# Layer 1's norm from x with features on partitions, in a two-layer retention / latent-attention trunk

## The chip, the cores and the metric

One core of a Trainium2 chip runs the whole program in one launch. The metric is the device time of one execution in microseconds (us). Engines are named as the profile names them: PE is TensorE's matrix products and PEld its weight loads, DVE is VectorE, ACT is ScalarE, POOL is GpSimd, SP is SyncE, which here only issues loads.

## The reference, cut to what matters

The model has two layers over a sequence of 512 tokens with 2048 features, batch 1. The first layer ("layer 1" in this document, index 0 in the code) is a retention layer, the second an attention layer. Each normalises x, shifts and scales it by vectors made from a conditioning vector c, and projects the result h.

```
def rmsnorm(x, g):
    y = x * rsqrt(mean(x * x, axis=-1) + EPS)          # one factor for each token
    return y * g

c_act = silu(c)
for i in range(2):
    shift, scale, gate = split(c_act @ ada_w[i] + ada_b[i], 3)
    h = rmsnorm(x, norm_g[i]) * (1.0 + scale) + shift
    y = retention_branch(h, ...) if i == 0 else mla_branch(h, ...)
    x = x + gate * y
return rmsnorm(x, final_norm_g)
```

In `retention_branch`, `h @ w_in` projects the 2048 features to q and k (2048 columns each), v and a gate g (4096 each). All is computed in float32; the kernel gets that precision on TensorE by splitting each operand into a high and a low part and adding three products (high x high, high x low, low x high).

## The kernel before, in words

The change concerns the first stage, which makes h for layer 1 and at the same time multiplies it with the first head's weights. h is held with features on partitions: 16 tiles `hT[kt]` of 128 features by 512 tokens, each with a high and a low half.

**Units.** The stage goes through 8 units of two tiles (kt = 2u and 2u+1). In each unit three sets of weights are used: "qk" (4 PSUM banks of results), "v" (4 banks) and "g" (3 banks). `products(kind, kt)` issues, for each bank, the three products of one tile; a unit has 24 + 18 + 24 = 66 products of 512 columns. There are eight PSUM banks (4 called `acc`, 4 called `aux`). The g banks stay; qk and v take turns in the four `acc` banks: after the first set (`here`) and g, `swap` copies its four partial results to SBUF (L379) and copies the other set's back (L383), both on ScalarE, and then `bank_products` does the second set (`there`). The next unit begins with the set that is already in the banks.

**Preparing a unit.** While TensorE multiplies unit u, `prepare_ahead(u+1)` prepares the next one. In the order of issue it does the following: ScalarE casts the weights of `here` to their high part (L330); VectorE reduces one tile of the modulation matrix against c (`sum_mod`, L353, once for shift and once for scale of each kt), makes the low part of the last odd h (L246) and the low part of `here` (L332), and reduces the second modulation tile; then `make_first` makes two columns, `b_col` (L366) and `a_col` (L367), on VectorE, and ScalarE makes h twice from the transposed x (`make_h`, L243 and L245). Then follow g's cast and low part, the cast of `there`, and two more reductions. After `swap`, `prepare_behind` makes the odd tile's h and the low part of `there`.

**The norm of x.** x comes in with tokens on partitions, as eight loads (L428). `square(t)` sums the squares of each token along the free axis, one half on ScalarE (L463) and one on VectorE (L464). `rsqrt` (L126) makes the factor: one small operation on VectorE (L129) and a power on POOL (L131). `diagonal(t)` (L476) writes the factors onto a diagonal matrix, and `transpose(kt)` (L497) multiplies four 128 x 128 blocks of x with these diagonals on TensorE, which transposes and normalises at once; ScalarE copies the result to SBUF (L502). Six tiles are transposed before the first product, tile 6 and 7 within unit 0, and two more in each of units 1 to 4.

**Order.** `queued(f)` puts the instructions of f behind the last ones already issued on ScalarE, VectorE, TensorE and SP, so the program's order is the order of each engine's queue. Buffers are taken from rings; those that matter are the raw weights (3), the high and low weights (3 each for qk and v, 4 named `k4b` for g), the modulation tiles `aw` (4, of 1 MB) and the tiles `k4` (8, x transposed). A load on SP waits for its buffer, and so do all loads behind it.

Of the kernel before, what the change touches and what calls it, by code (L numbers as in the profile page):

```python
# [49 lines left out]
def hybrid_trunk_kernel(  # L50
# [44 lines left out]
    def big(name, dt=F32R):  # L95
        return base.tile([P, 2, T], dt, tag="big", bufs=16, name=name)
# [4 lines left out]
    def k4b(name, dt=F32R):  # L101
        return base.tile([P, 2, T], dt, tag="k4b", bufs=4, name=name)
# [10 lines left out]
    def small(name, n=1):  # L113
        return base.tile([P, n], F32, tag="small", bufs=24, name=name)
# [248 lines left out]
    def make_first(kt):  # L363

        k1 = slice(kt, kt + 1)
        DVE.tensor_add(b_col[0][:, k1], mods[kt, 0], bias_c[0][:, k1])  # L366
        DVE.scalar_tensor_tensor(  # L367
            out=a_col[0][:, k1], in0=mods[kt, 1], scalar=bias1[:, k1], in1=norm_c[0][:, k1], op0=ALU.add, op1=ALU.mult
        )
        hT[kt] = big(f"hT_{kt}")  # L370
        return make_h(0, kt, xT[kt // 2][:, kt % 2, :], hT[kt])

# [18 lines left out]
    def product(kind, kt, b, late):  # L391
        lhs, rhs = first_sets[kind][1](loaded[kind, kt // 2], kt, b)
        passes = [(0, 0), (0, 1), (1, 0)]
        low = passes.pop(2 if kind == "v" else 1)
        for i, j in (low,) if late else passes:
            PE.matmul(
                banks[kind][b], lhs[i], rhs[j], start=kt == 0 and i + j == 0, stop=kt == KD - 1 and late,
                skip_group_check=True,
            )

    def bank_products(kind, u):

        for b in range(first_sets[kind][0]):
            for kt in (2 * u, 2 * u + 1):
                for late in (False, True):
                    product(kind, kt, b, late)

    A_, V_, T_, S_ = (getattr(mybir.EngineType, e) for e in ("Activation", "DVE", "PE", "SP"))

# [10 lines left out]
    def queued(fn, *args):  # L420
        with behind(A_, V_, T_, S_):
            return fn(*args)


    xs = [[big(f"x_{t}_{j}", F32) for j in range(2)] for t in range(NT)]
    for t in range(NT):
        for j in range(2):
            nc.sync.dma_start(  # L428
                xs[t][j], x[t * P : (t + 1) * P, j * 1024 : (j + 1) * 1024].rearrange("p (a b) -> p a b", a=2)
            )  # L430
# [12 lines left out]
    mods[1, 0] = queued(load_mod, 1, 0)  # L443
    load_first("qk", 0)
# [11 lines left out]

    bias1 = l0p.tile([P, KD], F32, name="bias1")

    ss = [small(f"x_ss_{t}", 2) for t in range(NT)]
    norm = [None] * NT  # L460

    def square(t):
        ACT.activation(k4b(f"x_sq_{t}_0", F32), xs[t][0], AF.Square, accum_out=ss[t][:, 0:1])  # L463
        DVE.scalar_tensor_tensor(  # L464
            out=k4b(f"x_sq_{t}_1", F32), in0=xs[t][1], scalar=1.0, in1=xs[t][1], op0=ALU.mult, op1=ALU.mult,
            accum_out=ss[t][:, 1:2],
        )
        s1 = small(f"x_s1_{t}")
        DVE.tensor_add(s1, ss[t][:, 0:1], ss[t][:, 1:2])
        norm[t] = rsqrt(s1, 1, 1.0 / D, f"x_{t}")  # L470

    diags = []

    def diagonal(t):
        diags.append(l0p.tile([P, P], F32, tag="diag", bufs=4, name=f"x_diag{t}"))
        DVE.tensor_scalar(out=diags[t], in0=ident, scalar1=norm[t], scalar2=None, op0=ALU.mult)  # L476

    tables_d = dram.tile([4 * P, T], F32, name="tables_d")
    ret_tables = [rot(l0p, f"ret_{n}") for n in ("cos", "sin")]
    tables = rotary_tables(*ret_tables, 0, False, "ret", ACT)  # L480
    for t in range(NT):
        queued(square, t)
        queued(silu, t)
        if t > 0:
            queued(diagonal, t - 1)
    queued(diagonal, NT - 1)
    POOL.dma_start(c_d, c_all[0:1, :])
    low_v = queued(prepares["v", 0])
    queued(lambda: DVE.tensor_scalar(out=bias1, in0=bias_c[0][:, KD:], scalar1=1.0, scalar2=None, op0=ALU.add))

    xT = [k4(f"xT_{u}", F32) for u in range(NU)]

    def transpose(kt):

        ps = aux(f"xT_ps_{kt}")
        for t in range(NT):
            PE.matmul(  # L497
                ps[:, t * P : (t + 1) * P],
                xs[t][kt // 8][:, (kt % 8) // 4, (kt % 4) * P : (kt % 4 + 1) * P],
                diags[t], start=True, stop=True,  # L500
            )
        return lambda: ACT.copy(xT[kt // 2][:, kt % 2, :], ps)  # L502
# [48 lines left out]
    queued(sum_mod, 1, 1)  # L551
    swap(None, "v")
    queued(products, "v", 0)
# [4 lines left out]
    queued(products, "qk", 0)  # L558
    prepare_ahead(1, low)
    queued(products, "qk", 1)  # L560
    queued(queued(transpose, 6))
    queued(products, "g", 1)
    queued(swap, "qk", "v")
    low = prepare_behind(1)
    queued(queued(transpose, 7))
    queued(products, "v", 1)
    for u in range(1, NU):

        here, there = ("qk", "v") if u % 2 == 0 else ("v", "qk")
        more = u + 1 < NU  # L570
        ahead = [2 * u + 6, 2 * u + 7] if 2 * u + 7 < KD else []
        if more:
            load_unit(u + 1)
            prepare_ahead(u + 1, low)
# [6 lines left out]
        for kt in ahead[:1]:  # L581
            queued(queued(transpose, kt))
        for kt in (2 * u, 2 * u + 1):
            queued(products, "g", kt)
        if more:
# [13 lines left out]
        for kt in ahead[1:]:  # L599
            queued(queued(transpose, kt))  # L600
    qk0, g0 = banks["qk"], banks["g"]
    l0.__exit__(None, None, None)

# [1569 lines left out]
```

## Time and profile before

| what | value |
|---|---|
| median of 3 runs | 2192.07 us (2192.05 to 2193.84) |
| profiled execution: its own time | 2192.7 us |
| its span | 2190.9 us |
| PE busy | 2160.2 us (99%) |
| DVE busy | 1557.4 us (71%) |
| ACT busy | 1013.1 us (46%) |
| POOL busy | 102.5 us (5%) |
| DMA moved | 440.26 MB, mean 201 GB/s |
| transposes of x | 64 products of 128 x 128, 128 instructions, 12.3 to 116.2 us |
| first product of v | 26.16 us |
| last product of the first stage | 161.42 us |

The span is the time from the first to the last instruction in the profile; the run's time lies 1.8 us around it. A busy share is the mean over stages with different limits, so the change has to be read in its own stage, the first 162 us. In lines of the timeline the first two numbers are the start and the length in us, the brackets give how long the engine had been idle and what ended that; "x8" counts instructions that follow each other. Lines of groups give the count, the total in us, the mean in ns and the idle time ahead.

### The profile page before, as it was taken

What the parts mean: (1) busy time and instruction counts of PE and PEld (TensorE: products, weight loads), DVE (VectorE), ACT (ScalarE), POOL (GpSimd) and SP (SyncE); (2) the same over time, 40 slices, a digit from 0 to 9 for tenths busy, and PEclk for the clock granted to TensorE, in tenths of its full rate; (3) what the DMA queues carried; (4) which work ended last, traced back from release to release, by engine and by line L of the source; (5) the groups of instructions that cost most, each with busy time, mean ns of one, the idle gap of its engine ahead of it and who ended that gap; (6) DMA issues with size and microseconds to landing.
All of it is one profiled execution on the core that took longest, in us unless ns stands there. A gap on an engine that the chain in (4) does not pass through costs nothing.

```text
span 2190.9 us, 27827 instructions
## 1 busy us (share of the span) xinstructions
PE 2160.2 (99%) x10280; PEld 1805.1 (82%) x10280; DVE 1557.4 (71%) x2345; ACT 1013.1 (46%) x1529; POOL 102.5 (5%) x178
## 2 busy tenths in 40 slices
PE   7999999999999999999999999999999999999997
PEld 5887888888888878888888888898788889888887
DVE  7878867676676788756677767667877677776545
ACT  5664434434343444434344545344444366664443
POOL 0000000000000000010000000010000000000000
PEclk9999999999999999999999999999999999999998
DMA  9965785867768678574645556453458723235323
GB/s 382 346 246 166 231 295 181 271 214 238 247 197 278 220 256 293 184 244 150 229 156 210 171 190 203 146 161 115 156 192 301 266 87 99 83 113 178 115 99 133
DMA packets 206907, 440.26 MB, mean 201 GB/s; under 512 B 19329, under 2 KB 60321, under 8 KB 202929
## 3 DMA queue, kind: packets, MB, share of 16 engines
q1 hardware_dynamic: 194560, 399.30, 54.7%
q0 software_dynamic: 11920, 38.91, 4.5%
q8 instruction: 80, 1.31, 0.2%
q14 instruction: 57, 0.47, 0.1%
q10 hardware_dynamic: 290, 0.27, 0.0%
HBM read 395.42 MB, written 43.00 MB: 200 GB/s over the span
## 4 chain that ended last, share of the span: by engine, by line
PE 81%; DVE 6%; issue 6%; ACT 3%; DMA 3%; POOL 0%; SPq 0%; POOLq 0%; DVEq 0%; ACTq 0%
PE o L1183 13%; PE qk L163 4%; PE qk L161 4%; PE qk L162 4%; PE o L2039 4%; PE x L729 2%; PE y L729 2%; PE y L730 2%; PE y L728 2%; PE x L730 2%; PE s L729 2%; PE s L730 2%; PE x L728 2%; PE s L728 2%; PE o L162 2%
## 5 line engine op out<-in xcount | busy, mean ns | idle before, releaser
L1183 PE MATMUL o<-o_h,o_whi 128*128 128x512 f32 (+1 forms) x496 | 192.2, 388 | 0.0
L1183 PE MATMUL o<-o_h,o_wlo 128*128 128x512 f32 (+1 forms) x496 | 191.4, 386 | 0.0
L1183 PE MATMUL o<-o_l,o_whi 128*128 128x512 f32 (+1 forms) x496 | 191.3, 386 | 0.0
L163 PE MATMUL qk<-hT,qk_l 128*128 128x512 f32 x448 | 174.9, 390 | 0.5 <-DVE qk_l L136 0.5
L161 PE MATMUL qk<-hT,qk_h 128*128 128x512 f32 x448 | 174.6, 390 | 0.0
L162 PE MATMUL qk<-hT,qk_h 128*128 128x512 f32 x448 | 174.4, 389 | 0.0
L136 DVE TENSOR_TENSOR o_wlo<-o_r,o_whi 128x1024 fp32r<-128x1024 f32 x61 | 74.6, 1223 | 84.1 <-ACT o_whi L135 84.1
L136 DVE TENSOR_TENSOR qk_l<-qk_r,qk_h 128x1024 fp32r<-128x1024 f32 x56 | 68.1, 1224 | 63.7 <-ACT qk_h L135 63.7
L1183 PEld LDWEIGHTS o<-o_h,o_wlo 128*128 128x128 f32 x496 | 93.2, 188 | 18.7
L1183 PEld LDWEIGHTS o<-o_l,o_whi 128*128 128x128 f32 x496 | 93.2, 188 | 18.3
L1183 PEld LDWEIGHTS o<-o_h,o_whi 128*128 128x128 f32 x496 | 93.2, 188 | 18.3
L163 PEld LDWEIGHTS qk<-hT,qk_l 128*128 128x128 f32 x448 | 84.1, 188 | 19.6 <-DVE qk_l L136 2.1
L162 PEld LDWEIGHTS qk<-hT,qk_h 128*128 128x128 f32 x448 | 84.1, 188 | 17.5
L161 PEld LDWEIGHTS qk<-hT,qk_h 128*128 128x128 f32 x448 | 84.1, 188 | 17.4
L135 ACT CAST qk_h<-qk_r 128x1024 fp32r<-128x1024 f32 x56 | 58.0, 1051 | 85.5 <-PE qk L162 62.0
L161 PE MATMUL g<-h,g_h 128*128 128x512 f32 x232 | 90.6, 390 | 0.3 <-ACT g_h L135 0.3
L162 PE MATMUL g<-h,g_h 128*128 128x512 f32 x232 | 90.3, 389 | 0.0
L885 DVE SCALAR_TENSOR_TENSOR mod<-mod,c_bm 128x1024 f32<-128x1024 f32 x64 | 78.1, 1220 | 16.6 <-DMA mod<-in_ada_t_dram 16.5
L163 PE MATMUL g<-h,g_l 128*128 128x512 f32 x232 | 89.8, 389 | 0.0
L353 DVE SCALAR_TENSOR_TENSOR aw<-aw,c_all 128x2048 f32<-128x2048 f32 (+1 forms) x34 | 73.3, 2161 | 2.8 <-DMA aw<-in_ada_t_dram 2.8
L135 ACT CAST o_whi<-o_r 128x1024 fp32r<-128x1024 f32 x61 | 63.6, 1054 | 23.5 <-issue 10.0
L136 DVE TENSOR_TENSOR o_w_lo<-o_w_raw,o_w_hi 128x1024 fp32r<-128x1024 f32 x32 | 39.0, 1221 | 36.7 <-ACT o_w_hi L135 36.6
(1261 smaller groups left out, 6028.4 us busy)
## 6 DMA issues: line engine op xcount, KB each, us to landing
mod<-in_ada_t_dram SPq DMA_DIRECT2D x128, 512.0 KB, 5.8
o_r<-in_ret_w_out_dram SPq DMA_DIRECT2D x64, 512.0 KB, 4.3
aw<-in_ada_t_dram SPq DMA_DIRECT2D x30, 1024.0 KB, 9.0
qk_r<-in_ret_w_in_dram SPq DMA_DIRECT2D x112, 256.0 KB, 4.1
g_r<-in_mla_w_in_dram SPq DMA_DIRECT2D x32, 512.0 KB, 4.4
o_w_raw<-in_mla_w_out_dram SPq DMA_DIRECT2D x32, 512.0 KB, 3.6
qk_d<-qk_st POOLq DMA_DIRECT2D x32, 256.0 KB, 3.7
qk_r<-qk_d SPq DMA_DIRECT2D x32, 256.0 KB, 5.8
```

The lines of the kernel that those rows point to most:

```text
L135: ACT.copy(hi, src)
L136: DVE.tensor_sub(lo, src, hi.bitcast(F32))
L161: PE.matmul(o, lhs[0], rhs[0], start=first and not seeded, stop=False, skip_group_check=seeded)
L162: PE.matmul(o, lhs[0], rhs[1], start=False, stop=False, skip_group_check=seeded)
L163: return PE.matmul(o, lhs[1], rhs[0], start=False, stop=last, skip_group_check=seeded)
L353: DVE.scalar_tensor_tensor(out=aw[:, cols], in0=aw[:, cols], scalar=1.0, in1=c_all[:, cols], op0=ALU.mult, op1=ALU.mult, accum_out=col[:, ...
L728: PE.matmul(banks[b], a[0], w[0], start=first, stop=False, skip_group_check=True)
L729: PE.matmul(banks[b], a[0], w[1], start=False, stop=False, skip_group_check=True)
L730: PE.matmul(banks[b], a[1], w[0], start=False, stop=True, skip_group_check=True)
L885: DVE.scalar_tensor_tensor(out=aw, in0=aw, scalar=1.0, in1=silu_c[j], op0=ALU.mult, op1=ALU.mult, accum_out=mc[:, j, b : b + 1],)
L1183: PE.matmul(o, w[i][:, ki, c0 + b * P : c0 + (b + 1) * P], a[j], start=first and i + j == 0, stop=last and i == 1, skip_group_check=True,)
L2039: PE.matmul(banks2[b][:, cols], w[0][i][:, 0, b * P : (b + 1) * P], o2_moving(w, u, cols)[j], start=u + i + j == 0, stop=u == KD - 1 and i ...
```

## The change

The host hands over x transposed and in units: `x_t` has the shape (8, 128, 2, 512), so that each of the eight tiles of x, two kt's with features on partitions, is one load with 4 KB in a row for each partition. The load of the residual in layer 1 reads the same array at the new place.

The squares are made on tiles with features on partitions, on ScalarE (even units) and VectorE (odd ones). VectorE adds the two kt's of a unit (`fold`), and TensorE sums over partitions: `add_squares` takes 128 tokens of the folded squares as weights and a column of ones as the moving operand, four products for each unit, collecting in one PSUM tile `x_sums` (four columns). The last unit's two halves are added without a fold, each with its own four products. `rsqrt` reads `x_sums`. The four columns of factors are written on diagonals by ScalarE and spread to all partitions by a product with ones (`spread_one`), into a PSUM tile `x_r` of 128 x 512 that stays to the end of the stage. `normalise(u)` multiplies a whole unit of x, two kt's, in place by `x_r` on VectorE (for unit 0 in two halves). Transposes, diagonals and evictions of the old form go.

Besides, `make_first` makes `b_col` and `a_col` on ScalarE and not on VectorE (the constant part of `a_col` is folded into `bias1` once, in `scaled_bias`); the three passes of `products` run pass by pass over all banks; the first modulation tiles are loaded ahead of v's first weights; and the start of unit 0 is ordered anew.

```
     def make_first(kt):
         k1 = slice(kt, kt + 1)
-        DVE.tensor_add(b_col[0][:, k1], mods[kt, 0], bias_c[0][:, k1])
-        DVE.scalar_tensor_tensor(
-            out=a_col[0][:, k1], in0=mods[kt, 1], scalar=bias1[:, k1], in1=norm_c[0][:, k1], op0=ALU.add, op1=ALU.mult
-        )
+        ACT.activation(b_col[0][:, k1], mods[kt, 0], AF.Identity, bias=bias_c[0][:, k1])
+        ACT.activation(a_col[0][:, k1], mods[kt, 1], AF.Identity, bias=bias1[:, k1], scale=norm_c[0][:, k1])
...
     def products(kind, kt):
-        for late in (False, True):
+        for n in range(3):
             for b in range(first_sets[kind][0]):
-                product(kind, kt, b, late)
+                product(kind, kt, b, n)
...
-    xs = [[big(f"x_{t}_{j}", F32) for j in range(2)] for t in range(NT)]
-    for t in range(NT):
-        for j in range(2):
-            nc.sync.dma_start(
-                xs[t][j], x[t * P : (t + 1) * P, j * 1024 : (j + 1) * 1024].rearrange("p (a b) -> p a b", a=2)
-            )
+    xT = [k4(f"x_{u}", F32) for u in range(NU)]
+    for u in range(NU):
+        for j in (0, 1) if u == NU - 1 else (slice(0, 2),):
+            nc.sync.dma_start(xT[u][:, j, :], x_t[u, :, j, :])
...
+    load_mods(0)
     load_first("v", 0)
-    load_mods(0)
...
+    x_sums = aux("x_sums")
+    sq = {}
+    def square(u, j=slice(0, 2)):
+        if u not in sq:
+            sq[u] = k4b(f"x_sq_{u}", F32)
+        o, i = sq[u][:, j, :], xT[u][:, j, :]
+        if u % 2 and u < NU - 1:
+            DVE.tensor_mul(o, i, i)
+        else:
+            ACT.activation(o, i, AF.Square)
+    def fold(u):
+        DVE.tensor_add(sq[u][:, 0, :], sq[u][:, 0, :], sq[u][:, 1, :])
+    def add_squares(u, j=0):
+        for t in range(NT):
+            PE.matmul(
+                x_sums[:, t : t + 1], sq[u][:, j, t * P : (t + 1) * P], crow, start=u + t == 0, stop=u + j == NU,
+                skip_group_check=True,
+            )
...
+    for u in range(NU - 1):
+        queued(square, u)
+        if u < 4:
+            queued(silu, u)
+        if u % 2:
+            queued(fold, u - 1)
+            queued(fold, u)
+            queued(add_squares, u - 1)
+            queued(add_squares, u)
+    for j in range(2):
+        queued(square, NU - 1, j)
+    queued(fold, NU - 2)
+    queued(add_squares, NU - 1, 0)
+    queued(add_squares, NU - 2)
+    queued(add_squares, NU - 1, 1)
+    r_col = queued(rsqrt, x_sums[:, 0:NT], NT, 1.0 / D, "x")
...
+    def spread_one(t):
+        cols = slice(t * P, (t + 1) * P)
+        ACT.activation(diag[:, cols], ident, AF.Identity, scale=r_col[:, t : t + 1])
+        PE.matmul(x_r[:, cols], ones, diag[:, cols], start=True, stop=True)
+    def normalise(u, j=None):
+        v = xT[u] if j is None else xT[u][:, j, :]
+        r = x_r.unsqueeze(1).to_broadcast([P, 2, T]) if j is None else x_r
+        DVE.tensor_mul(v, v, r)
...
+    queued(scaled_bias)
+    queued(sum_mod, 0, 0)
     for t in range(NT):
+        queued(spread_one, t)
+    queued(normalise, 0, 0)
+    queued(sum_mod, 0, 1)
     low_v = queued(prepares["v", 0])
+    low = queued(make_first, 0)
+    queued(low_v)
+    queued(low)
-    for kt in range(6):
-        queued(queued(transpose, kt))
...
     def prepare_ahead(u, first=None):
...
         queued(low)
+        queued(normalise, u)
         queued(sum_mod, 2 * u, 1)
         low = queued(make_first, 2 * u)
...
     load_unit(1)
-    queued(low_v)
-    for s in range(2):
-        queued(sum_mod, 0, s)
-    low = queued(make_first, 0)
+    queued(queued(prepares["g", 0]))
+    queued(normalise, 0, 1)
     queued(sum_mod, 1, 0)
-    queued(low)
-    lows = [queued(prepares[kind, 0]) for kind in ("g", "qk")]
-    for low in lows:
-        queued(low)
+    queued(queued(prepares["qk", 0]))
     queued(sum_mod, 1, 1)
...
-        nc.sync.dma_start(o1_res[b, r], x_t[kt * P : (kt + 1) * P, :])
+        nc.sync.dma_start(o1_res[b, r], x_t[kt // 2, :, kt % 2, :])
```

More of the change, by code (lines that the diff above doesn't have):

```diff
@@ L404, in bank_products @@
             for kt in (2 * u, 2 * u + 1):
-                for late in (False, True):
-                    product(kind, kt, b, late)
+                for n in range(3):
+                    product(kind, kt, b, n)
     A_, V_, T_, S_ = (getattr(mybir.EngineType, e) for e in ("Activation", "DVE", "PE", "SP"))
@@ L457, in hybrid_trunk_kernel @@
     bias1 = l0p.tile([P, KD], F32, name="bias1")
[L459 to L476, printed above, removed]
+    x_sums = aux("x_sums")
[12 more added lines that the diff above has]
+        for t in range(NT):
+            PE.matmul(
+                x_sums[:, t : t + 1], sq[u][:, j, t * P : (t + 1) * P], crow, start=u + t == 0, stop=u + j == NU,
+                skip_group_check=True,
+            )
     tables_d = dram.tile([4 * P, T], F32, name="tables_d")
@@ L480, in hybrid_trunk_kernel, with scaled_bias @@
     tables = rotary_tables(*ret_tables, 0, False, "ret", ACT)
-    for t in range(NT):
[L482 to L487, printed above, removed]
-    low_v = queued(prepares["v", 0])
[L489 to L502, printed above, removed]
-    for kt in range(6):
-        queued(queued(transpose, kt))
+    for u in range(NU - 1):
[14 more added lines that the diff above has]
+    r_col = queued(rsqrt, x_sums[:, 0:NT], NT, 1.0 / D, "x")
+    POOL.dma_start(c_d, c_all[0:1, :])
+    diag = tmp("x_diag")
+    x_r = aux("x_r")
+    def spread_one(t):
[6 more added lines that the diff above has]
+        DVE.tensor_mul(v, v, r)
+    def scaled_bias():
+        DVE.scalar_tensor_tensor(
+            out=bias1, in0=bias_c[0][:, KD:], scalar=1.0, in1=norm_c[0], op0=ALU.add, op1=ALU.mult
+        )
+    queued(scaled_bias)
+    queued(sum_mod, 0, 0)
+    for t in range(NT):
+        queued(spread_one, t)
+    queued(normalise, 0, 0)
+    queued(sum_mod, 0, 1)
+    low_v = queued(prepares["v", 0])
+    low = queued(make_first, 0)
+    queued(low_v)
+    queued(low)
     def load_unit(u):
@@ L580, in hybrid_trunk_kernel @@
             queued(products, here, kt)
-        for kt in ahead[:1]:
-            queued(queued(transpose, kt))
         for kt in (2 * u, 2 * u + 1):
```

18 lines of the change are left out of this document (4 added, 14 removed).

## The prediction

> **What bounds the kernel now.** I read the table of engines first, then the stretches of the first 60 us, then the chain that ended last from 0 to 80 us, then the waits of TensorE.
>
> ```profile
> PE 2160.2 (99%) x10280; PEld 1805.1 (82%) x10280; DVE 1557.4 (71%) x2345; ACT 1013.1 (46%) x1529; POOL 102.5 (5%) x178
> ...
> 0.00:20.00 20.00, 11.99 (x26) 6.52 (x27) 9.82 (x27) 10.83 (x16) 4.62 (x14) 1.00 0.90 342
> 20.00:40.00 20.00, 18.34 (x94) 15.45 (x93) 17.68 (x27) 11.37 (x18) 0.00 (x0) 1.00 1.04 404
> 40.00:60.00 20.00, 16.73 (x72) 13.43 (x73) 19.43 (x22) 15.78 (x25) 0.00 (x0) 0.91 1.02 407
> ```
>
> TensorE is busy for 99% of the span, and the three stretches hold its gaps: 12.0, 18.3 and 16.7 us of 20. In the second and third the queues move 404 and 407 GB/s and VectorE is busy for 17.7 and 19.4 us. So the ramp is crowded: DMA, VectorE and TensorE are all near full.
>
> ```profile
> 30.21 11.30 DMA qk_raw<-in_ret_w_in_dram
> ...
> 41.62 1.05 ACT qk_whi L330
> 42.66 0.48 ACT xT L502
> ...
> 48.03 6.42 PE v L396 x27
> ...
> 66.09 5.46 PE qk L396 x24
> 71.55 0.89 PE xT_ps L497 x8
> 72.44 4.10 PE g L396 x18
> ```
>
> The columns are start, length and what the chain ran through. Up to 41.6 us the chain hangs on a transfer, then on ScalarE's cast, one transpose's eviction and the exchange of banks (`swap`), and from 48.03 us on it is TensorE alone, with transposes of 0.89 us among the products.
>
> ```profile
> PE qk L396 <- ACT qk L383: 0.2, 1, 0.2
> ...
> 161.42 0.39 PE L396 MATMUL qk<-hT,qk_whi 128*128 128x512 f32 x1
> ```
>
> The first row is all that TensorE waited for between 48 and 160 us; the second is the last product of the stage. Hence a check of the model. Twenty-four products take 5.46 us (0.2275 each) and the 18 of g 4.10, so a unit is 2 x 5.46 + 4.10 = 15.02 us. At 48.03 us six products of unit 0 are left, so unit 1 begins at 49.4. Units 1 to 4 carry two transposed tiles each (16.80 us), units 5 to 7 none: 49.4 + 4 x 16.80 + 3 x 15.02 = 161.7, where 161.42 + 0.23 = 161.65 was measured. The stage's end is therefore the start of unit 1 plus seven units, and what follows is bound by TensorE and shifts with it. A gain needs one of two things: an earlier unit 1, or shorter units that nothing else stretches.
>
> **The change, first part: the sums of squares move to TensorE, and VectorE waits for them.** The eight tiles of x still come first. Squares and folds are ready soon after x lands (their four buffers for eight tiles come free as the sums go, which costs no more than the sums do), but the sums stand on TensorE behind the eight instructions that spread c:
>
> ```profile
> 5.24 7.16 PE L422 MATMUL c_ps<-c_all,ones 1*128 1x512 f32 x8 [5.24 <-DMA c_all<-in_c_dram]
> ...
> 8.34 0.57 POOL L131 TENSOR_TENSOR x_r<-x_v,mhalf 128x1 f32<-128x1 f32 x1 [5.95 <-DVE x_v L129]
> ...
> 16.68 8.09 PE L497 MATMUL xT_ps<-x_diag,x 128*128 128x128 f32 x44 [1.78 <-DVE x_diag L476]
> ...
> 18.30 0.59 ACT L502 COPY xT<-xT_ps 128x512 f32<-128x512 f32 x1 [1.17 <-PE xT_ps L497]
> 20.01 0.59 ACT L502 COPY xT<-xT_ps 128x512 f32<-128x512 f32 x1 [1.12 <-PE xT_ps L497]
> 21.71 0.59 ACT L502 COPY xT<-xT_ps 128x512 f32<-128x512 f32 x1 [1.12 <-PE xT_ps L497]
> 23.02 0.59 ACT L502 COPY xT<-xT_ps 128x512 f32<-128x512 f32 x1 [0.72 <-PE xT_ps L497]
> ...
> 2167.34 0.53 PEld L2069 LDWEIGHTS x_sums<-ones,x_ss 128*128 128x128 f32 x4
> ...
> L2069 PEld LDWEIGHTS x_sums<-ones,x_ss x8: 186/192/192, 2167.3 to 2178.4; 128*128 128x128 f32 x8
> L2069 PE MATMUL x_sums<-ones,x_ss x8: 164/250/271, 2167.5 to 2178.5; 128*128 128x1 f32 x8
> ```
>
> They begin at 5.24 + 7.16 = 12.40 us. There are nine groups of four products with one column each (36), and TensorE runs an f32 product as two instructions (44 here for 22 transposes), so 72. The price of one: the nearest row is the kernel's last norm, the same form with a warm clock, four weight loads in 0.53 us where one is 0.19 (186/192/192 ns): (0.53 - 0.19) / 3 = 0.113 us. Warm transposes cost the same, 0.89 / 8 = 0.111, so it is the weight load that paces both. Cold transposes took (20.01 - 18.30) / 8 = 0.213. Which clock holds? The c products streamed for 7.16 us without a pause and still left it cold: the transposes begun at 16.68 ran at the cold pace until after 21.71, when the copies draw together (1.71, then 1.31 us). A product with one row in use warmed nothing, and one with a single column keeps as little of the array at work. So I take 0.213: 72 x 0.213 = 15.3, sums done at 27.7, their reader `x_v` at 27.9. Bounds: 20.7 all warm, 30.6 at 0.25, the median length of one such product, as if nothing overlapped.
>
> That reader is VectorE's, in `rsqrt`, and behind it in the queue stand `scaled_bias`, `sum_mod(0,0)`, half a normalise, `sum_mod(0,1)` and everything after. Before, all that ran from 17 us, as the loads landed. Their lengths, start to start where the engine had no gap:
>
> ```profile
> 17.33 0.17 DVE L489 TENSOR_SCALAR bias<-vcol 128x16 f32<-128x16 f32 x1
> 18.54 1.22 DVE L353 SCALAR_TENSOR_TENSOR aw<-aw,c_all 128x1024 f32<-128x1024 f32 x1
> 21.02 1.22 DVE L353 SCALAR_TENSOR_TENSOR aw<-aw,c_all 128x1024 f32<-128x1024 f32 x1
> ...
> 27.04 0.69 DVE L246 TENSOR_TENSOR hT<-h_0f,hT 128x512 fp32r<-128x512 f32 x1
> 27.65 0.95 DVE L332 TENSOR_TENSOR g_k4b<-g_raw,g_k4b 128x768 fp32r<-128x768 f32 x1
> 28.53 1.23 DVE L332 TENSOR_TENSOR qk_wlo<-qk_raw,qk_whi 128x1024 fp32r<-128x1024 f32 x1
> 29.67 2.28 DVE L353 SCALAR_TENSOR_TENSOR aw<-aw,c_all 128x2048 f32<-128x2048 f32 x1
> ...
> 32.59 2.29 DVE L353 SCALAR_TENSOR_TENSOR aw<-aw,c_all 128x2048 f32<-128x2048 f32 x1 [0.37 <-DMA aw<-in_ada_t_dram]
> ```
>
> That the `ada` loads now precede v's costs nothing: all of them have landed by then. From 27.9: `x_v` and the bias, two like the 0.17, 0.3; `sum_mod(0,0)` 2.48 (18.54 to 21.02), to 30.7. Beside it run the root on POOL (0.57) and four diagonals on ScalarE with their spreads; at 0.40 each (row L1750 below) and two cold instructions, 0.57 + 4 x 0.40 + 0.43 = 2.6, so the cover about holds; I add nothing, and without cover 2.6. Half a normalise 0.61, `sum_mod(0,1)` 2.48, to 33.8. Now ScalarE makes the two columns (0.6, below) and both copies of h (0.82 and 0.80 in the rows below, 0.1 overlapping, as VectorE's do: 1.14 from start to start for a length of 1.23), over v's low part on VectorE, to 35.9; h low 0.61, g low 0.88, half a normalise 0.61, `sum_mod(1,0)` 2.21, qk low 1.14, `sum_mod(1,1)` 2.21: 43.6. There `sum_mod(2,0)` starts, which before started at 32.59, held by its transfer alone. **Shift: +11.0 us.** The first products start late with it, which costs nothing by itself. SP's queue stands too: unit 1's first load waits for v's raw buffer, freed only when v's low part is made, near 35 us; it and the next tile of `ada` (1.57 MB at 404 GB/s, 3.9 us) still land before 43.6, so DMA sets nothing here.
>
> **Second part: from there to unit 1.** Before, 32.59 to 49.4. Added: `normalise(1)` ahead of `sum_mod(2,1)`, 1.14; the columns on ScalarE, 0.3 (both below); v's low part, which finds its cast (1.06) begun only with h's low part (0.61), 0.36 after the overlap; and pass-major products, so that after the last bank is back nine products remain and not six, 3 x 0.2275 = 0.68. Gone: the eviction of a transpose ahead of the exchange, 0.48, and the end of the wait for the transfer, 30.21 + 11.30 = 41.51, about 0.2. **+1.8 us.**
>
> **Third part: seven units.** The transposes go, 8 x 0.89 = 7.1 us. Whether a unit falls to 15.02 depends on the loop through ScalarE and VectorE, best seen in unit 6, which has no transposes:
>
> ```profile
> 131.90 1.06 ACT L330 CAST v_whi<-v_raw 128x1024 fp32r<-128x1024 f32 x1 [0.64 <-PE qk L396]
> 132.99 1.23 DVE L332 TENSOR_TENSOR v_wlo<-v_raw,v_whi 128x1024 fp32r<-128x1024 f32 x1 [1.00 <-ACT v_whi L330]
> 134.13 2.29 DVE L353 SCALAR_TENSOR_TENSOR aw<-aw,c_all 128x2048 f32<-128x2048 f32 x1
> 136.34 0.08 DVE L353 DVE_READ_ACCUMULATOR aw<-aw,c_all 128x1 f32 x1
> 136.72 0.82 ACT L243 ACTIVATE hT<-xT,b_col,a_col 128x512 fp32r<-128x512 f32 x1 [3.76 <-DVE a_col L367]
> ...
> 145.41 0.80 ACT L245 ACTIVATE h_15f<-xT,b_col,a_col 128x512 f32<-128x512 f32 x1
> ...
> L2093 DVE TENSOR_TENSOR y<-x,x_r 128x512 f32<-128x512 f32 x14 | 8.8, 679 | 1.1 <-PE x_r L931 1.1
> L463 ACT ACTIVATION_READ_ACCUMULATOR x_sq<-x 128x1 f32 x4 | 0.7, 187 | 0.0
> L1750 ACT ACTIVATE p<-p,rs 128x128 f32<-128x128 f32 x8 | 3.2, 404 | 3.9 <-DVE rs L1744 3.9
> ```
>
> The cast at 131.90 waited 0.64 us for TensorE to free a weight buffer. From it the loop runs: low part, `sum_mod`, columns, h, g's cast, the next cast, eight copies of the exchange, h of the odd tile, finished, less the overlap, at 146.1; then the next cast can start. That is 14.2 us, 0.8 under TensorE's 15.02. The change puts into it: `normalise(u)`, 1024 columns with one operand in PSUM. The row L2093 has 0.679 for 512 columns; 512 more cost 0.53 in SBUF (1.22 against 0.69 in the rows above), so about 1.21, and 1.14 start to start like the row at 132.99. And the columns: on VectorE 0.38 from 136.34 to 136.72, with the odd pair off the loop; on ScalarE both pairs lie on it. No row has an ACTIVATE of one column; the nearest are 0.187 (reading the accumulator) and 0.404 (128 columns, one pointer operand), so a pair lies between 0.37 and 0.81; I take 0.6. Even pair: 0.08 (the accumulator's read comes first) + 0.6 - 0.38 = 0.3 more, odd pair 0.6. The loop becomes 14.2 + 1.14 + 0.3 + 0.6 = **16.24 us, which exceeds TensorE's 15.02**. TensorE then stands idle at each exchange. Six units of 16.24 and the last of 15.02 make 112.5, against 112.3 before: the transposes' 7.1 us are eaten entirely, **+0.2 us**. (ScalarE: Activation LUTs in the Trainium skill, section What ACT_TABLE_LOAD costs, prices such a pair at 0.28 and 0.37 us with 0.09 overlap; with its 0.56 the sum would fall by half a microsecond.)
>
> The residual's load in layer 1 still fetches 2 KB runs, at another stride: nothing.
>
> Sum: 11.0 + 1.8 + 0.2 = +13.0 on the profiled run's 2192.7 us (span 2190.9), so 2205.7; the median of the runs lies 0.6 lower: **2205.1 us**.
>
> **Rivals.** (1) *The clock warms during the sums.* As with the transposes, 5.5 us in: 26 instructions cold, 46 x 0.113 = 5.2, sums read at 23.3 instead of 27.9: -4.6, 2200.5 us. For it: the array is fed without a gap. Against: the c products. Chance 0.24. The page TensorE: Matmul & The Clock Gate of the Trainium skill, Part 1, says the clock doubles after about 3.4 us of sustained activity; by that rule the sums end near 22 and the time is about 2199.3. The trace agrees for the transposes within two of its windows, not for the c products.
> (2) *The loop doesn't bind*, since the normalise slips into a gap of VectorE: units of 15.02, 6 x 1.22 less, 2197.8 us. For: VectorE waited 1.0 us before 132.99. Against: that gap lies ahead of the cast, not behind. Chance 0.10.
> (3) *Not slower: the sums hide behind x's loading.* If a one-column product is paced by its column, not by its load, the 72 are done by 16.9 us, the point up to which VectorE keeps its old start at 32.59; that takes 0.06 us each. Then 1.8 + 0.2 is left: 2194.1 us. Against: the warm row's 0.113. Chance 0.08.
> (4) (2) and (3) together, the change doing what its removal of the transposes suggests: about 2186.8 us. Chance 0.03.
>
> **The numbers.** The forecast has 0.55. About 0.2% (4.4 us) is what a measurement of this kernel can tell from no change. The range runs from rival (2) with half a microsecond off, 2197, to the slower weight load (72 x 0.25, +2.7) and a pair at its upper bound (0.2 x 13, +2.6) in part: 2209. Slower 0.86 (forecast, 1 and 2, less a tail of 0.03), same 0.10 (mostly 3), faster 0.04.
>
> **What would show it.** Right: 72 one-column products from 12.4 to about 27.7; `x_v` idle before it until TensorE; first product of v near 35 us rather than 26.16; hT's ScalarE starts for even tiles about 16.2 us apart; TensorE waiting about 1.2 us for `swap` in each of six units; stage end near 175. Wrong: sums done by 17 us; even tiles 15.0 us apart; the wait of VectorE for x gone without another in its place.

## The result, and the profile after

The changed kernel takes **2207.68 us** (median of four runs, 2206.63 to 2208.59), the kernel before, timed beside it, 2192.38 us (four runs, 2192.05 to 2193.84): ratio 1.0068, 95% interval 1.0051 to 1.0086. 2205.1 us and slower had been forecast. The profiled execution has a span of 2206.5 us, 15.6 more than before.

The table of engines and the stretches of the first 60 us (length, then busy us of PE, PEld, DVE, ACT and POOL, each with its number of instructions, then PEclk, the clock granted to TensorE as a share of full speed, the share of DMA and GB/s):

```profile
PE 2162.7 (98%) x10232; PEld 1806.3 (82%) x10232; DVE 1562.9 (71%) x2313; ACT 1014.6 (46%) x1547; POOL 101.9 (5%) x175
...
0.00:20.00 20.00, 15.05 (x46) 10.45 (x46) 8.25 (x12) 10.01 (x12) 2.33 (x10) 1.00 0.93 352
20.00:40.00 20.00, 12.67 (x51) 11.74 (x52) 9.30 (x18) 6.19 (x12) 2.03 (x1) 1.00 0.49 176
40.00:60.00 20.00, 13.57 (x52) 10.02 (x52) 19.87 (x20) 12.06 (x21) 0.00 (x0) 0.85 1.03 403
```

The table would not have shown the change: TensorE is still busy for 98%, with more work and not less. The stretches do. Between 20 and 40 us VectorE fell from 17.7 busy us to 9.3 and the queues from 404 to 176 GB/s: for about half of that time both stand and wait for something else.

What it is stands in the timelines of TensorE, VectorE and POOL (start, length, group, and in brackets the idle time before it with what ended it):

```profile
4.95 7.16 PE L417 MATMUL c_ps<-c_all,ones 1*128 1x512 f32 x8 [4.95 <-DMA c_all<-in_c_dram]
12.04 15.52 PE L471 MATMUL x_sums<-ones,x_sq 128*128 128x1 f32 x72
27.59 0.16 DVE L129 TENSOR_SCALAR x_v<-x_sums 128x4 f32<-128x4 f32 x1 [8.46 <-PE x_sums L471]
27.84 2.03 POOL L131 TENSOR_TENSOR x_r<-x_v,mhalf 128x4 f32<-128x4 f32 x1 [14.28 <-DVE bias L510]
30.36 2.08 PE L502 MATMUL x_r<-x_diag,ones 128*128 128x128 f32 x8 [2.80 <-ACT x_diag L501]
32.47 0.69 DVE L507 TENSOR_TENSOR x<-x,x_r 128x512 f32<-128x512 f32 x1 [2.15 <-PE x_r L502]
...
45.40 2.29 DVE L353 SCALAR_TENSOR_TENSOR aw<-aw,c_all 128x2048 f32<-128x2048 f32 x1
```

The 72 one-column instructions take 15.52 us, 0.2155 each, directly behind the c products; VectorE has been idle for 8.46 us when `x_v` runs. Two more steps in a row follow, POOL's root (2.03 us) and the spread, and the first normalise starts at 32.47. `sum_mod(2,0)`, at 32.59 before, starts at 45.40: **+12.8 us**.

In the units the chain that ended last, which ran on TensorE alone before, now goes round through three engines (start, length, what it ran through; between 90 and 113 us):

```profile
90.39 5.79 PE v L392 x24
96.20 1.06 ACT qk_whi L330
...
98.43 1.22 DVE x L507
99.65 2.22 DVE aw L353 x2
...
106.02 0.60 ACT qk L381
...
106.66 5.77 PE qk L392 x24
112.45 1.07 ACT v_whi L330
```

One turn, cast, low part, normalise, `sum_mod`, columns, h, the next cast, the first bank back, 24 products that free the buffer for the cast, takes 112.45 - 96.20 = 16.25 us, and the starts of h for even tiles lie 16.24 apart in all units (86.04, 102.31, 118.56, 134.80, 151.03). The loop of the prediction, by way of the odd tile's h, runs beside it and is nearly as long, as the timelines of VectorE and ScalarE in unit 6 show:

```profile
128.67 0.69 DVE L246 TENSOR_TENSOR hT<-h_11f,hT 128x512 fp32r<-128x512 f32 x1 [1.31 <-ACT h_11f L245]
...
130.92 1.22 DVE L507 TENSOR_TENSOR x<-x,x_r 128x1024 f32<-128x1024 f32 x1
132.05 2.29 DVE L353 SCALAR_TENSOR_TENSOR aw<-aw,c_all 128x2048 f32<-128x2048 f32 x1
134.26 0.08 DVE L353 DVE_READ_ACCUMULATOR aw<-aw,c_all 128x1 f32 x1
...
134.38 0.39 ACT L367 ACTIVATE a_col<-mc,bias,vcol 128x1 f32<-128x1 f32 x1 [4.44 <-DVE aw L353]
134.80 0.82 ACT L243 ACTIVATE hT<-x,b_col,a_col 128x512 fp32r<-128x512 f32 x1
...
142.76 0.29 ACT L366 ACTIVATE b_col<-mc,vcol 128x1 f32<-128x1 f32 x1
142.96 0.37 ACT L367 ACTIVATE a_col<-mc,bias,vcol 128x1 f32<-128x1 f32 x1
143.36 0.81 ACT L243 ACTIVATE hT<-x,b_col,a_col 128x512 fp32r<-128x512 f32 x1
144.08 0.80 ACT L245 ACTIVATE h_13f<-x,b_col,a_col 128x512 f32<-128x512 f32 x1
144.92 1.06 ACT L330 CAST v_whi<-v_raw 128x1024 fp32r<-128x1024 f32 x1
```

TensorE needs 15.02 and waits for the rest, by the waits of TensorE from 20 to 180 us (us in total, times, the longest) and its timeline at the end of the stage:

```profile
PE v L392 <- ACT v L381: 8.9, 4, 5.9
PE qk L392 <- ACT qk L381: 2.6, 3, 1.0
...
175.92 0.40 PE L161 MATMUL g<-hT,g_h 128*128 128x512 f32 x1
```

Without the one of 5.9 us in the ramp, v's exchanges cost 1.0 us each and qk's 0.9. The first product after the stage comes at 175.92, 161.64 before: **+14.28 us**. Unit 1 begins at 63.46 and not at 48.83 (the lines are under *To unit 1* below), 14.63 us later. So all of the loss is made in the first 64 us, and the seven units, freed of 7.1 us of transposes, take 112.46 us where they took 112.81: only 0.35 us of the 7.1 is gained.

### The profile page after: what moved, and what is told of

Same layout as the page of the kernel before. It is cut to its first block, busy times and chain, and to the rows that moved or that the text cites. A ratio compares the mean times of both kernels' runs of the same rounds, so it can differ in the third digit from the quotient of the medians.

```text
span 2206.5 us, 27730 instructions
## 1 busy us (share of the span) xinstructions
PE 2162.7 (98%) x10232; PEld 1806.3 (82%) x10232; DVE 1562.9 (71%) x2313; ACT 1014.6 (46%) x1547; POOL 101.9 (5%) x175
## 3 DMA queue, kind: packets, MB, share of 16 engines
q8 instruction: 80, 1.31, 0.3%
## 4 chain that ended last, share of the span: by engine, by line
PE 80%; DVE 8%; issue 4%; ACT 4%; DMA 2%; POOL 0%; SPq 0%; DVEq 0%; POOLq 0%; ACTq 0%
PE o L1191 13%; PE qk L163 4%; PE qk L162 4%; PE qk L161 4%; PE o L2047 4%; PE x L737 2%; PE y L737 2%; PE y L738 2%; PE y L736 2%; PE x L738 2%; PE s L737 2%; PE s L738 2%; PE x L736 2%; PE s L736 2%; PE g L161 2%
## 5 line engine op out<-in xcount | busy, mean ns | idle before, releaser
L161 PE MATMUL qk<-hT,qk_h 128*128 128x512 f32 x448 | 174.5, 390 | 0.0
L161 PEld LDWEIGHTS qk<-hT,qk_h 128*128 128x128 f32 x448 | 84.1, 188 | 17.5
L161 PE MATMUL g<-h,g_h 128*128 128x512 f32 x232 | 90.6, 390 | 0.3 <-ACT g_h L135 0.3
```

The lines of the kernel that those rows point to most:

```text
L161: PE.matmul(o, lhs[0], rhs[0], start=first and not seeded, stop=False, skip_group_check=seeded)
```

## The experiments

"Stage end" below is the start of the first product of L161 (175.92 above), or the end of the last product ahead of it where that one waits. The theory is that of the prediction: the cold sums hold VectorE's queue (first part), then a loop through ScalarE and VectorE sets the units (third part). Each experiment takes one piece out, or several. A ratio is to the kernel before, timed with the experiment.

**e1: the columns back on VectorE.**

```
-    ACT.activation(b_col[0][:, k1], mods[kt, 0], AF.Identity, bias=bias_c[0][:, k1])
-    ACT.activation(a_col[0][:, k1], mods[kt, 1], AF.Identity, bias=bias1[:, k1], scale=norm_c[0][:, k1])
+    DVE.tensor_add(b_col[0][:, k1], mods[kt, 0], bias_c[0][:, k1])
+    DVE.scalar_tensor_tensor(out=a_col[0][:, k1], in0=mods[kt, 1], scalar=norm_c[0][:, k1],
+                             in1=bias1[:, k1], op0=ALU.mult, op1=ALU.add)
```

> The changed kernel, with b_col and a_col made on VectorE again. Theory (the loop through ScalarE and VectorE sets the units, and both pairs of columns lie on it): even tiles of hT start about 15.4 us apart and not 16.24, six units give 5 us, and the start of unit 0 about 0.5 us: 2202 us. Rival (the loop is set by the normalise and the transfers, and the small operations hide): no change, 2207.7 us.

Measured: 2205.20 us, ratio to the kernel before 1.0054 (1.0038 to 1.0071). Even tiles 16.08 apart, not 15.4; stage end 174.57. A miss in size: of the 0.9 us that the columns were thought to cost in a unit, only the even pair's 0.16 came back. ScalarE's timeline says why:

```profile
126.23 0.80 ACT L245 ACTIVATE h_11f<-x,b_col,a_col 128x512 f32<-128x512 f32 x1
127.67 1.05 ACT L330 CAST qk_whi<-qk_raw 128x1024 fp32r<-128x1024 f32 x1 [0.63 <-PE v L394]
```

The cast of the next weights stands behind the odd h, and with the odd pair gone from ScalarE that is done earlier; but now the cast waits 0.63 us for TensorE to free the buffer. The turn by way of the 24 products, seen in the chain above, doesn't pass the odd pair. It does pass the normalise.

**e2: the normalise moved into VectorE's gap.** In the changed kernel VectorE waits 1.31 us for the odd h before it makes its low part (128.67 above), and the normalise stands behind the two low parts.

```
         queued(sum_mod, 2 * u, 0)
+        queued(normalise, u)
         if first is not None:
             queued(first)
         queued(low)
-        queued(normalise, u)
         queued(sum_mod, 2 * u, 1)
```

> The changed kernel, with the normalise of the next unit put ahead of the low part of the odd h, that is, into the 1.3 us for which VectorE waits for ScalarE in each unit. Same work, another place. Theory (the normalise costs because it lies on the loop, not because VectorE is full: its work is about 14.3 us in a unit): even tiles 15.1 us apart, six units give 6.8 us: 2201 us. Rival (VectorE is the bound by its sum of work): no change or under 1 us.

Measured: 2202.21 us, ratio 1.0038 (1.0023 to 1.0053). Even tiles 67.96, 83.08, 98.18, 113.29, 128.40, 143.50, so 15.1 apart; stage end 168.42, 7.5 us earlier than in the changed kernel. VectorE's timeline:

```profile
122.00 1.22 DVE L507 TENSOR_TENSOR x<-x,x_r 128x1024 f32<-128x1024 f32 x1
123.42 0.69 DVE L246 TENSOR_TENSOR hT<-h_11f,hT 128x512 fp32r<-128x512 f32 x1 [0.20 <-ACT h_11f L245]
124.50 1.23 DVE L332 TENSOR_TENSOR qk_wlo<-qk_raw,qk_whi 128x1024 fp32r<-128x1024 f32 x1 [0.39 <-ACT qk_whi L330]
```

The normalise now ends 0.2 us before the odd h is there, so it costs nothing. With units of 15.1 it is shown that the transposes' gain was eaten by the normalise's *place*, not by its length.

**e3: three reductions ahead of the reader of the sums.** `scaled_bias`, sum_mod(0,0) and sum_mod(0,1) are put ahead of `rsqrt`, and sum_mod(1,0) right behind it.

```
+    queued(scaled_bias)
+    queued(sum_mod, 0, 0)
+    queued(sum_mod, 0, 1)
     r_col = queued(rsqrt, x_sums[:, 0:NT], NT, 1.0 / D, "x")
...
-    queued(scaled_bias)
-    queued(sum_mod, 0, 0)
+    queued(sum_mod, 1, 0)
     for t in range(NT):
         queued(spread_one, t)
     queued(normalise, 0, 0)
-    queued(sum_mod, 0, 1)
...
     queued(normalise, 0, 1)
-    queued(sum_mod, 1, 0)
```

> The changed kernel, with the reductions of kt 0 and the first of kt 1 put ahead of VectorE's wait for the sums of squares (the reader x_v). Theory (the late sums cost because VectorE's queue stands behind their reader): sum_mod(2,0) starts near 40.3 us and not 45.4, all of it reaches the end: 2202.6 us. Rival (transfers or TensorE's first products set the start of unit 1): under 1 us.

Measured: 2203.61 us, ratio 1.0045 (1.0030 to 1.0060); sum_mod(2,0) at 41.53, stage end 171.62, 4.3 us earlier than in the changed kernel. So work that needs no sum, but stood behind their reader in VectorE's queue, made 4.3 of the 14.3 us; the rest of the delay at the start hangs on `x_v` itself (e5). The theory had put sum_mod(2,0) at 40.3. Part was lost again: the normalise came only at 33.39, since POOL's root took long (e10):

```profile
27.79 3.01 POOL L131 TENSOR_TENSOR x_r<-x_v,mhalf 128x4 f32<-128x4 f32 x1 [14.28 <-DVE x_v L129]
```

**e4: TensorE warmed ahead of the sums** by 20 dense f32 products of 128 columns, whose result is not used.

```
+    def warm():
+        PE.matmul(x_sums[:, P : 2 * P], ident, ones, start=True, stop=True, skip_group_check=True)
+    for _ in range(20):
+        queued(warm)
```

> The changed kernel, with 20 dense products of 128 columns (no use is made of them) between the spreading of c and the sums of squares. They should take 7 us, cold for 5.5 of them. If a stream of one-column products keeps a warm clock, the 72 then run at 0.113 us, x_v comes near 27.5 us as before and the time stays at 2207.7 us. If the stream lets the clock fall again after a while, x_v comes at 30 us or later and the time rises by 2.5 us or more; if the weight loads take 0.213 us whatever the clock, by 7 us.

Measured: 2211.47 us, ratio 1.0082 (1.0067 to 1.0097); `x_v` at 30.54, stage end 178.78, 2.9 us later than in the changed kernel: the second of the three cases, a clock that falls again. Stretches of 2 us of this run, columns as above (the second is TensorE's products; a stretch counts every instruction that reaches into it):

```profile
16.00:18.00 2.00, 2.00 (x21) 2.00 (x20) 0.00 (x0) 0.00 (x0) 0.00 (x0) 1.00 1.04 412
18.00:20.00 2.00, 2.00 (x21) 2.00 (x20) 0.04 (x1) 0.93 (x1) 0.00 (x0) 1.00 1.01 394
20.00:22.00 2.00, 1.87 (x17) 1.78 (x17) 2.00 (x3) 1.27 (x3) 0.00 (x0) 0.98 1.10 428
22.00:24.00 2.00, 2.00 (x11) 2.00 (x11) 1.00 (x2) 0.95 (x2) 0.00 (x0) 0.50 0.98 380
24.00:26.00 2.00, 2.00 (x11) 2.00 (x11) 0.00 (x0) 0.00 (x0) 0.00 (x0) 0.50 1.13 411
```

The dense products, begun at 12.10, do warm the clock within about 3 us: 6 instructions between 14 and 15 us, 11 between 15 and 16, 21 in 2 us from 16 us on. The sums begin at 18.08, at first at that pace. Within 4 us the granted clock falls to 0.50 and the pace to 11 in 2 us, though TensorE has been idle for only 0.13 us. This stream of one-column products keeps no warm clock, and by the 15.52 us of the changed kernel it makes none.

**e5: fewer products.** All squares on ScalarE, added on VectorE over the tiles as they come, the two halves at the end; four products (eight instructions) are left of 36.

```
+    def fold(u):
+        DVE.tensor_add(sq[0], sq[0], sq[u])
+    def add_squares():
+        DVE.tensor_add(sq[0][:, 0, :], sq[0][:, 0, :], sq[0][:, 1, :])
+        for t in range(NT):
+            PE.matmul(x_sums[:, t : t + 1], sq[0][:, 0, t * P : (t + 1) * P], crow, start=t == 0, ...)
```

> The changed kernel, with all squares made on ScalarE and added up over the eight units on VectorE, so that TensorE sums one tile with 4 products (8 instructions) and not 36 (72). Theory (the 72 cold weight loads set x_v, and x_v sets the start): x_v near 20 us and not 27.6, all of it reaches the end: about 2200.2 us, ratio to before 1.0034. Rival (the transfers of the first unit's weights and modulation tiles set the start): x_v is earlier but the time falls by under 2 us.

Measured: 2201.36 us, ratio 1.0042 (1.0028 to 1.0056); `x_v` at 21.78, normalise at 26.66, sum_mod(2,0) at 39.59, stage end 169.80, 6.1 us earlier than in the changed kernel. `x_v` comes 5.8 us earlier and all of that arrives at the end of the stage: in the changed kernel's order the sums are on the path one for one.

**e6 and e7: all four together (e1, e2, e3, e5),** and in e7 also the old order of the passes of `products`:

```
-        for n in range(3):
+        for ns in ((0, 1), (2,)):
             for b in range(first_sets[kind][0]):
-                product(kind, kt, b, n)
+                for n in ns:
+                    product(kind, kt, b, n)
```

> The changed kernel with four edits at once: columns on VectorE, normalise ahead of the odd h's low part, the reductions of kt 0 and 1 ahead of x_v, and the squares added up on VectorE. Theory: x_v near 20 us, sum_mod(2,0) near 34.5 us (1.9 later than before), units of 15.02 us bound by TensorE, so that the transposes' 7.1 us are gained: 5 us under the kernel before, ratio 0.9976. Rival (VectorE is the bound in the units, with about 14.9 us of work in 15.0): units of 15.5 us or more and no gain over before.

> The four edits, and the order of passes in products as in the kernel before. Theory: 0.7 us under the run with the four edits, by the three products fewer behind the last bank of the first exchange; within the noise of the times, so to be read from the start of unit 1. Rival: no difference.

Measured: e6 2192.45 us, ratio 0.9999 (0.9990 to 1.0008), stage end 161.18; e7 2192.25 us, 0.9996 (0.9987 to 1.0005), 160.92. The order of the passes is worth 0.3 us, not the 0.7 expected. The loss is gone, but the gain expected is not there. The units do what was forecast: even tiles from 46.35 to 136.23 in six steps, 14.98 each, which is TensorE's own pace. The start does not, by VectorE's and POOL's timelines of e6:

```profile
24.57 0.15 DVE L129 TENSOR_SCALAR x_v<-x_sums 128x4 f32<-128x4 f32 x1
24.64 2.28 DVE L353 SCALAR_TENSOR_TENSOR aw<-aw,c_all 128x2048 f32<-128x2048 f32 x1
...
24.81 3.01 POOL L131 TENSOR_TENSOR x_r<-x_v,mhalf 128x4 f32<-128x4 f32 x1 [11.31 <-DVE x_v L129]
...
30.42 0.69 DVE L505 TENSOR_TENSOR x<-x,x_r 128x512 f32<-128x512 f32 x1 [3.48 <-PE x_r L500]
...
38.69 2.29 DVE L353 SCALAR_TENSOR_TENSOR aw<-aw,c_all 128x2048 f32<-128x2048 f32 x1
```

The sums were done at 21.5, but their reader stood behind sum_mod(0,1) until 24.57, an order that was right for e3's late sums and wrong for e5's early ones; then the root took 3.01 us beside a sum of 2048 columns. sum_mod(2,0) starts at 38.69 and not at 34.5.

**e8: the kernel before with the columns on ScalarE alone,** made as in the changed kernel (`bias1` with the constant part folded in).

```
-        DVE.tensor_add(b_col[0][:, k1], mods[kt, 0], bias_c[0][:, k1])
-        DVE.scalar_tensor_tensor(out=a_col[0][:, k1], in0=mods[kt, 1], scalar=bias1[:, k1],
-                                 in1=norm_c[0][:, k1], op0=ALU.add, op1=ALU.mult)
+        ACT.activation(b_col[0][:, k1], mods[kt, 0], AF.Identity, bias=bias_c[0][:, k1])
+        ACT.activation(a_col[0][:, k1], mods[kt, 1], AF.Identity, bias=bias1[:, k1], scale=norm_c[0][:, k1])
```

> The kernel BEFORE, with b_col and a_col on ScalarE and nothing else of the change. Theory (the loop there has 14.2 us, and the columns add 0.8, which stays at TensorE's 15.02 or below): under 1 us of difference. Rival (ScalarE's columns cost their length in each unit): 7 units of 0.6 to 0.8 us, 4 to 5 us slower.

Measured: 2196.11 us, ratio 1.0017 (1.0008 to 1.0026), more than expected. The 4 us are near the rival's number, but not by its mechanism: even tiles lie 16.97 apart where 16.79 stood before, 0.18 a unit and not 0.6 to 0.8, and the stage ends at 163.05, 1.4 us later. The other 2.6 us appear between 220 and 871 us, where the two programs are the same: near 855 us VectorE waits 2.75 us for a load of the modulation matrix (0.56 in the kernel before), and TensorE then 1.4 us for VectorE. Why that load comes late stays open (below).

**e9: the reader of the sums between sum_mod(0,0) and sum_mod(0,1),** on top of e7.

```
     queued(sum_mod, 0, 0)
-    queued(sum_mod, 0, 1)
     r_col = queued(rsqrt, x_sums[:, 0:NT], NT, 1.0 / D, "x")
+    queued(sum_mod, 0, 1)
```

> The kernel of e7_all_four_pass with one move: the reader of the sums (`x_v`, in `rsqrt`) stands on VectorE between sum_mod(0,0) and sum_mod(0,1), not behind both. Theory: what kept e6 and e7 from a gain is that `x_v` stood in VectorE's queue until 24.6 us although its sums were done by 21.7, and that POOL's root beside a 2048-wide sum took 3.01 us. Here `x_v` at about 22.1, the root beside 1024-wide sums 2.0 us, the first normalise at about 27 instead of 30.4, sum_mod(2,0) at 35.2 instead of 38.7, stage end at 157.5 instead of 160.9, and a time 3 to 4 us below the kernel before: ratio about 0.9982. Rival: the start no longer hangs on VectorE's queue but on transfers (v's buffer for unit 1, the next tile of ada), so that sum_mod(2,0) or unit 1's cast wait for a DMA and the stage ends within 1 us of 160.9: ratio 0.9996.

Measured: **2189.06 us** (11 runs, 2186.30 to 2189.93), before 2192.61 (15 runs): ratio **0.9983, 0.9974 to 0.9992**, faster than both kernels. VectorE, POOL and TensorE:

```profile
22.09 0.15 DVE L129 TENSOR_SCALAR x_v<-x_sums 128x4 f32<-128x4 f32 x1
22.16 1.21 DVE L353 SCALAR_TENSOR_TENSOR aw<-aw,c_all 128x1024 f32<-128x1024 f32 x1
22.33 1.94 POOL L131 TENSOR_TENSOR x_r<-x_v,mhalf 128x4 f32<-128x4 f32 x1 [8.82 <-DVE x_v L129]
26.87 0.69 DVE L506 TENSOR_TENSOR x<-x,x_r 128x512 f32<-128x512 f32 x1
...
35.18 2.29 DVE L353 SCALAR_TENSOR_TENSOR aw<-aw,c_all 128x2048 f32<-128x2048 f32 x1
...
157.43 0.39 PE L161 MATMUL g<-hT,g_h 128*128 128x512 f32 x1
```

Every step came where it was put: normalise at 26.87 without a wait, sum_mod(2,0) at 35.18, stage end at 157.43, 4.2 us before that of the kernel before, and the span is 4.2 us shorter (2186.7). The rival, a start bound by transfers, fell. So 4.2 of the transposes' 7.1 us can be saved; the changed kernel gave them back through its 72 one-column products and its order of work.

**e10: VectorE left idle beside POOL's root.** As e3, with sum_mod(1,0) in its old place; against e3:

```
-    queued(sum_mod, 1, 0)
     for t in range(NT):
         queued(spread_one, t)
...
     queued(normalise, 0, 1)
+    queued(sum_mod, 1, 0)
```

> The kernel of e3_sums_first with sum_mod(1,0) put back to its old place behind the first normalise, so that VectorE has nothing to do while POOL takes the root of four columns (3.01 us there, 2.03 in the changed kernel). Theory: the root's length is stretched by the VectorE operation that runs beside it; with VectorE idle it takes about 1.0 us, as the eight roots of the same shape later in the kernel do on average, and the first normalise starts near 31.4 instead of 33.4. Rival: the length is the operation's own at this place (a first use, or POOL's queue), and it takes 2 to 3 us again, normalise at 32.5 or later.

Measured in one run: 2203.64 us. POOL's timeline:

```profile
27.85 1.03 POOL L131 TENSOR_TENSOR x_r<-x_v,mhalf 128x4 f32<-128x4 f32 x1 [14.28 <-DVE x_v L129]
```

1.03 us, with the same queue, place and operands for which e3 showed 3.01, and the normalise comes at 31.49. The length beyond 1.03 us is made by the VectorE operation beside it. As a remedy it is worth nothing here: sum_mod(1,0), moved behind the normalise, has to run anyway, sum_mod(2,0) stays at 41.57 (41.53 in e3), and the stage ends at 171.74 (171.62).

## Why the prediction was right, step by step

*The sums.* 72 instructions at the cold pace, right: 15.52 us for 15.3, `x_v` at 27.59 for 27.9. The reason given, that one column keeps too little of the array at work to warm it, was an analogy to the c products. e4 shows directly that the stream neither makes nor keeps a warm clock. Its dense products load weights of the same 128 x 128 and differ in the moving columns, 128 against 1; what it is in that difference that counts is not shown. The rule quoted in rival (1), from TensorE: Matmul & The Clock Gate of the Trainium skill, Part 1, counts sustained activity: e4's dense products agree with it (warm within about 3 us), the 15.5 us of one-column products don't. Rivals (1) and (3) fell with this step; e5 and e9 show that where the sums are early, VectorE is early.

*The queue behind them.* Right in its mechanism (e3), 1.8 us short in size, and the step that failed is the cover of the spread: "the cover about holds; I add nothing, and without cover 2.6". The root was taken as 0.57 us from a row with one column; it took 2.03. It began 0.25 us after `x_v`, and diagonals and spread took 2.60 us to the normalise where 2.03 had been allowed. sum_mod(0,0), the cover, ended at 30.3, and VectorE then waited 2.15 us, so the normalise came at 32.47 and not at 30.7. From there to sum_mod(2,0) 12.93 us passed, 12.9 had been worked out.

*To unit 1.* 1.8 us had been put down. TensorE's timeline and the stretches, in each pair first the kernel before, then the changed one:

```profile
48.60 0.62 PE L396 MATMUL v<-v_whi,hT 128*128 128x512 f32 x2
62.61 2.31 PE L392 MATMUL v<-v_whi,hT 128*128 128x512 f32 x6
...
48.00:50.00 2.00, 1.97 (x9) 1.62 (x10) 1.96 (x1) 2.00 (x4) 0.00 (x0) 1.00 1.07 414
62.00:64.00 2.00, 2.00 (x6) 1.52 (x6) 0.69 (x3) 1.81 (x3) 0.00 (x0) 0.50 0.93 331
```

The twelve products of unit 0's odd tile begin at 44.92 and at 57.79; the thirteenth, which begins unit 1, is the second of the two at 48.60, at 48.83, and the third of the six at 62.61, at 63.46. So the prediction's 49.4 was a misreading: the 27 products from 48.03 on are three of unit 0, not six, and the 24 of unit 1. Its sum of 161.7 still met the measured 161.65, because the seven units together took 0.55 more than their sum.

From sum_mod(2,0) to unit 1 it is 18.06 us now and 16.24 before: 1.8 more, as put down, but that is luck. ScalarE's first copy back of the exchange (43.67, now 57.15) comes 0.67 later against sum_mod(2,0), where the terms ahead of it add up to 1.1. The other 1.15 lie between that copy and unit 1, where 0.68 stood for nine products behind the last bank instead of six. By the trace four remain instead of three, but each takes 0.42 us: behind a wait of 5.93 us TensorE's granted clock is 0.50 from 54 to 64 us, while before it read 1.00 from 48 us on. The prediction had no such term.

*The units.* Forecast 16.24, measured 16.24, but not by the forecast's loop alone, and that the two agree to the hundredth is luck. That loop, 14.2 us before, gains 1.13 for the normalise, 0.16 for the even pair (0.54 from 134.26 to 134.80, where 0.38 stood before; not 0.3, because `b_col` is made well ahead) and 0.60 for the odd pair (142.76 to 143.36): 16.09. The cast then comes 0.84 us behind the start of the odd h where 0.70 had been allowed, since the other turn, through the 24 products and the weight buffer, is longer by those 0.14. It makes up for the 0.14 by which the even pair had been put too high. Two turns lie that close together; the prediction had only one of them, and e1 shows that the odd pair, 0.6 in its sum, is not on the one that binds. The lengths that ScalarE: Activation LUTs in the Trainium skill, section What ACT_TABLE_LOAD costs, gave for a pair (0.28 and 0.37) agree with the rows, 0.29 and 0.37 to 0.39. Rival (2) fell as the change stands, and e2 turns it into a remedy: the gap of 1.0 us ahead of the low part, which was said to lie on the wrong side of the cast, is not the one that serves; another, of 1.31 us, opens ahead of the odd tile's low part. The forecast of +0.2 for the seven units came out as -0.35, since the kernel before took 112.81 for them and not 112.3.

*Sum.* Forecast 11.0 + 1.8 + 0.2 = 13.0; measured 12.8 + 1.8 - 0.35 = 14.3 at the end of the stage. The span grew by 15.6, so 1.3 us came later. "What follows is bound by TensorE and shifts with it" holds only so far: at the stage's end, at 871, 1745 and 2008 us the changed kernel lies 14.3, 14.8, 13.9 and 16.1 us behind. In the last of these stretches a product of the second layer waits 1.8 us for VectorE (at 1972 us; 1.7 us in e2), which it does not do in the kernel before. Other variants drift too (e2 by +3.0 from the stage's end to the end, e5 +0.7, e1 -0.5, e9 0.0; e8's wait at 855 us is of this kind), and single runs of one kernel differ by 2 us and more (2190.73 to 2195.22 in 27 runs of the kernel before). Nothing was tried on it; why these waits come and go is open.

## What to carry to other kernels

Work that is taken off the bounding engine pays only as far as nothing else has been placed in its stead on the path: here 7.1 us of transposes went, and a reduction at the head of VectorE's queue plus 1.1 us in the wrong place of a loop cost more. Ask of each added instruction not only how long it is, but which gap of its engine it falls into, and put a reader of late data behind the work that doesn't need it, just as far as the data are late (e3, e6, e9). A reduction over partitions by products with one column cost 0.2155 us an instruction here, two for each product, and did not warm the clock; fold first on other engines, then do few of them (e5).

## What the runs showed of the hardware

**POOL's root waits for the VectorE operation beside it.** The same root of 128 x 4 took 1.03 us beside an idle VectorE (e10), 1.94 to 2.03 beside a reduction of 1024 columns that had just begun (changed kernel, e5, e9), and 3.01 beside one of 2048 (e3, e6). In all five of the latter cases it ends 0.90 us after that VectorE operation: in e6, 24.64 + 2.28 = 26.92 and 24.81 + 3.01 = 27.82; in e9, 22.16 + 1.21 = 23.37 and 24.27. The next VectorE operation, which in the changed kernel starts at 28.90, before the root's end at 29.87, doesn't stretch it. SBUF — State Buffer in the Trainium skill, section Who interferes with whom, says that a VectorE instruction with two SBUF inputs, as `sum_mod` is, contends with a GpSimd instruction that reads SBUF; these rows agree.

**The clock's column can show 1.00 while the pace is half.** In the changed kernel PEclk reads 1.00 through the 15.5 us of the sums:

```profile
14.00:16.00 2.00, 2.00 (x11) 2.00 (x11) 0.35 (x1) 1.00 (x1) 0.00 (x0) 1.00 1.00 387
```

That is 11 instructions in 2 us. e4 reads 0.50 at the same pace (22 to 26 us above), once its clock had been warm. Until the first change of the clock the pace of a known instruction is the better witness.
